# The first norm's modulation by quarters of the features, with the v product behind each quarter

## The chip, the cores and the metric

The kernel runs on one core of one Trainium2 chip. The metric is the time on the device for one execution, in microseconds, here as the median of several runs. Five engines work beside each other: TensorE (PE in the profile) multiplies matrices, VectorE (DVE), ScalarE (ACT) and GpSimd (POOL) do the elementwise work, and SyncE (SP) issues the transfers (DMA) from memory. Each engine takes its instructions in the order of its own queue.

## What is computed

Three blocks of a transformer over 256 tokens of 1024 features, all in float32. The change lies in the beginning of the first one:

```
c_act = silu(c)                                    # one vector of 1024
mod   = c_act @ ada_w[0] + ada_b[0]                # 6 x 1024: sh1, sc1, g1, sh2, sc2, g2
h = rmsnorm(x, norm_g[0, 0]) * (1 + sc1) + sh1     # first norm and its modulation
q, k, v, o, ig, fg = split(h @ a_w_in)             # 512, 512, 1024, 1024, 8, 8
y = mlstm(q, k, v, gates ig and fg)                # 8 heads, chunks of 128 tokens
y = (sigmoid(o) * headnorm(y)) @ a_w_out
x = x + g1 * rmsnorm(y, norm_g[0, 1])              # then sh2, sc2, feed-forward, g2, ...
```

After this come a feed-forward, a second block with a gating unit and its feed-forward, and a third block with attention, a convolution and a mixture of experts. None of them is touched.

## The kernel before

Activations are kept transposed, features on the 128 partitions: `x` is 8 chunks of 128 features by 256 tokens. A float32 product is made of three faster ones: `split` (line 349) cuts an operand into a high part (ScalarE, line 350) and the rest (VectorE, line 351), and `mm3` (line 380) adds high x high, high x low and low x high. `dense_b` (line 392) makes one chunk of 128 output features for 256 tokens with 24 such products over 256 columns. `Acc` (line 54) makes an output with tokens on the partitions, 1024 features wide: 12 products over 512 columns for each of the 8 input chunks, into four PSUM tiles; the last `tail` chunks are held back and then done first for one half of the tokens and then for the other. `weights` (line 359) loads 1 MiB of weights into one of three buffers `st` of the pool `wst` and splits it in two halves.

The modulation vectors come from `ada_w`, 4 MiB each. The two that the first norm needs (sh1 and sc1) are made in `first_block` (line 825) by `ada_start` (line 463), four times 512 features: half of the 8 input chunks are multiplied and summed by VectorE (lines 477 and 479), the other half go through float32 products on TensorE against a replicated vector `crep` (line 481), a float32 product with ones adds the sum over partitions (line 482), and `diagonal` (line 486) picks the columns out of the replicated rows. Then `Finish.whole` (line 243) normalises x, transposes it, applies gain and shift, and runs a `Head` (line 117): float32 products, straight from the unsplit activations, of the 40 gate columns and the first two q chunks (line 135).

`mlstm` (line 584) goes on: gates (tanh, exp, log on ScalarE, then two scans on VectorE, lines 597 to 609), a round trip through memory that spreads the running maximum `M` over the partitions (lines 612 to 615), and its masking on GpSimd. The other q and k chunks follow as split products (lines 624 to 631), then the v product by `dense_a` (line 642), whose four PSUM tiles ScalarE copies to `v` (line 645). Then the o loop (line 694) runs the o product with two heads' scores and sums ahead of each pair of chunks, and the output product ends the block, with the next norm and the feed-forward's float32 head behind it.

The other modulation vectors of the block (g1, sh2, sc2) are side work: generators of steps. `pump(budget)` (line 280) runs steps as long as the budget is above zero; a step that loads 1 MiB and multiplies it on VectorE (line 507) counts 2.4, an adding step with TensorE (lines 535 and 517) 0.6 or 1.3. With a budget of 2.0, `mlstm` calls it after the third and the fourth pair of q and k chunks, four times in the v product and three times in the o loop. `ada_row` also loads a row of `norm_g` and one of the bias. All these loads use the three buffers of `wst`, and the transfers stand in SP's queue in the order in which the program makes them.

The order of the instructions on each engine is not written out by hand, apart from a few places (`issue_after`): a planner sets it before the run, from the order of the program and its own estimates of when an operand is ready.

Of the kernel before, what the change touches and what calls it, by code (L numbers as in the profile page):

```python
# [10 lines left out]
F32 = mybir.dt.float32  # L11
# [6 lines left out]
ALU = mybir.AluOpType  # L18
# [5 lines left out]
KD = 8  # L24
T = 256
# [112 lines left out]
class Finish:  # L138
# [101 lines left out]
            self.run(1)  # L240
            self.split(1)

    def whole(self):

        self.chain(0, None)
        self.turn(0)
        self.end(None)


class Lent:  # L250

# [9 lines left out]
class Net:  # L261
# [198 lines left out]
        return t  # L460


    def ada_start(self, i, b, o):


        nc = self.nc
        s = self.ada_p.tile([128, 1024], F32, tag="ada", name="ada")[:, :512]
        w = self.a["ada_w"][i, b // 2].rearrange("q p (k n) -> q p k n", k=2)[:, :, :, (b % 2) * 512:(b % 2 + 1) * 512]
        ps = self.sd_tile()
        for h in range(2):  # L470
            st = self.wst.tile([128, 2048], F32, tag="st", name="st").rearrange("p (k n) -> p k n", k=4)
            for q in range(2):
                nc.sync.dma_start(st[:, 2 * q:2 * q + 2], w[2 * h + q])
            for k in range(4):
                kk = 4 * h + k
                if kk == 1:
                    nc.vector.tensor_scalar(s, st[:, k], self.cact[:, kk:kk + 1], None, op0=ALU.mult)
                elif k % 2:
                    nc.vector.scalar_tensor_tensor(s, st[:, k], self.cact[:, kk:kk + 1], s, op0=ALU.mult, op1=ALU.add)
                else:  # L480
                    nc.tensor.matmul(ps, self.crep[:, kk], st[:, k], start=kk == 0, stop=False)
        nc.tensor.matmul(ps, self.ones, s, start=False, stop=True)
        self.diagonal(ps, o)
        nc.vector.tensor_tensor(o, o, self.col("ada_b", 48 * i + 4 * b, 4), op=ALU.add)

    def diagonal(self, ps, o):

        nc = self.nc
        d = self.ada_p.tile([128, 4, 128], F32, tag="adad", name="adad", bufs=1)
        nc.vector.tensor_tensor(d, ps.rearrange("p (k c) -> p k c", k=4), self.ident.unsqueeze(1).to_broadcast([128, 4, 128]), op=ALU.mult)  # L490
        nc.vector.tensor_reduce(o, d, axis=AX.X, op=ALU.add)
# [89 lines left out]
        return fin.x  # L581


    def mlstm(self, x, pump, finish):
        nc, a = self.nc, self.a
        with ExitStack() as es:
            mp = es.enter_context(self.tc.tile_pool(name="ml", bufs=1))
# [3 lines left out]
            v = mp.tile([128, 2, 8, 129], F32, name="v")  # L591
            nc.gpsimd.memset(v[:, :, :, 128:129], 1.0)
            one8 = mp.tile([8, T], F32, name="one8")
            nc.gpsimd.memset(one8, 1.0)

            ps = self.head.ps[0]
            b15 = mp.tile([40, 1], F32, name="b15")
            nc.vector.tensor_scalar(b15, self.col("bif")[:40], 1.0 / 15.0, None, op0=ALU.mult)
            th = mp.tile([40, T], F32, name="th")
# [16 lines left out]
            for o in (0, 256):  # L616
                d = mx[:, :, o:o + 128]
# [4 lines left out]

            kT = mp.tile([128, 4, T], F32, name="kT")
            for n2 in range(4):
                for j, ps in enumerate(self.pair(x, a["a_w_qk"], n2, 1)):
                    n = 2 * n2 + j
                    if n < 4:
                        nc.scalar.copy(qz[0:64, 2 * n], ps[0:64])
                        nc.scalar.copy(qz[64:128, 2 * n + 1], ps[64:128])  # L629
                    else:  # L630
                        nc.scalar.mul(kT[:, n - 4], ps, 0.125)
                if n2 == 2:
                    pt = self.sd_tile()
                    for t in range(2):
                        nc.tensor.transpose(pt[:, t * 8:t * 8 + 8], av[:, t * 128:(t + 1) * 128], self.ident[:8, :8])
                        nc.tensor.transpose(pt[:, 16 + t * 8:24 + t * 8], em[:, t * 128:(t + 1) * 128], self.ident[:8, :8])
                    ac = mp.tile([128, 4, 8], F32, name="ac")
                    nc.vector.tensor_copy(ac, pt[:, :32].rearrange("p (a h) -> p a h", a=4))
                if n2 >= 2:
                    self.pump(pump)  # L640

            acc = self.dense_a(x, a["a_w_v"], pump=pump)
            for t in range(2):
                for h in range(2):
                    nc.scalar.copy(v[:, t, 4 * h:4 * h + 4, :128], acc[t][h].rearrange("p (h d) -> p h d", h=4))
            hh = mp.tile([128, 2, 8, 129], F32, name="hh")
            sq = mp.tile([128, 2, 8], F32, name="sq")

# [44 lines left out]
            acc = Acc(self, KD, tail=3)  # L693
# [18 lines left out]
        with self.tc.tile_pool(name="work", bufs=1) as p:  # L712
            fin = finish(p)
# [111 lines left out]
    def first_block(self):  # L825
        with self.tc.tile_pool(name="adap", bufs=2) as self.ada_p, self.tc.tile_pool(name="wsx", bufs=2) as self.wsx:
            m0, first, rest = self.ada_mods(0)
            with self.tc.tile_pool(name="crep", bufs=1) as p:
                self.crep = p.tile([128, KD, 128], F32, name="crep")
                self.nc.vector.tensor_copy(self.crep, self.cact.unsqueeze(2).to_broadcast([128, KD, 128]))  # L830
                for b in range(4):
                    self.ada_start(0, b, m0["sh1" if b < 2 else "sc1"][:, 4 * (b % 2):4 * (b % 2) + 4])
                    if b == 0:
                        self.nc.sync.dma_start(self.X, self.a["x"].rearrange("o (t p) d -> p (o t) d", p=128))
                o = m0["sc1"]
                self.nc.vector.scalar_tensor_tensor(o, o, 1.0, self.col("ng0_0"), op0=ALU.add, op1=ALU.mult)
            with self.tc.tile_pool(name="st0", bufs=2) as p, self.tc.tile_pool(name="work", bufs=1) as work:
                fin = Finish(self, work, None, m0["sc1"], m0["sh1"], head=[(self.a["a_w_g"], 1, 40)] + self.pairs(self.a["a_w_qk"], 2), head_pool=p)
                fin.whole()
# [12 lines left out]
        self.wsx = None  # L852
        return x
# [573 lines left out]
def prep(i):  # L1427
    c = lambda v: np.asarray(v).reshape(-1, 128).T
# [22 lines left out]
    o["norm_g"], o["ada_b"] = i["norm_g"], i["ada_b"]  # L1451

    o["ada_w"] = i["ada_w"].reshape(2, 4, 2, 128, 6, 1024).transpose(0, 4, 1, 3, 2, 5).reshape(2, 6, 4, 128, 2048)
    o["ffn_w1"] = np.stack([_pack_b(w) for w in i["ffn_w1"]])
    o["ffn_w2"] = np.stack([_pack_a(w) for w in i["ffn_w2"]])
    w = i["a_w_in"][0]
    g = np.zeros((1024, 40), f32)
# [4 lines left out]
    w = i["b_w_in"][0]  # L1462
# [5 lines left out]
    w = i["w_in_2"][0]  # L1468
# [37 lines left out]
```

## Time and profile before

| | us |
|---|---|
| median of 3 runs | 1779.6 (1777.91 to 1779.66) |
| profiled execution | 1777.4 |
| its span, first to last instruction | 1775.7 |
| TensorE busy in the span | 1727.9 |
| VectorE busy | 1370.4 |
| ScalarE busy | 865.8 |

The profiled execution is one run, and the times of all rows are its times, counted from the start of its span. A busy time counts an engine's instructions that run, not whether it does useful work at its peak; matrix products overlap, so TensorE's busy time can be read as the time in which it had something to do. The last part of the page follows the chain of work that ended last back from the end of the span; an engine with a large share of it sets the time.

### The profile page before, as it was taken

The page shows a single profiled execution, that of the slowest core. Times are in us where ns is not written, and L with a number is a line of the kernel's source. Part 1 is how long each engine was busy: PE and PEld are TensorE (multiplying, and loading weights), DVE is VectorE, ACT ScalarE, POOL GpSimd, SP SyncE. Part 2 cuts the span into 40 slices and gives each one's busy share as a digit, 9 for nine tenths or more (in the row PEclk, how much of TensorE's full clock was granted, in tenths as well). Part 3 has the DMA queues.
Part 4 walks back from the last instruction along what each step waited for, and adds up shares of the span by engine and source line. Part 5 has one row for each costly group of instructions (what it writes and reads, how often), then busy time and mean ns, then how long its engine had stood idle before and what let it go on. Part 6 is the DMA issues. An engine that isn't in the chain of part 4 may idle for free.

```text
span 1775.7 us, 29680 instructions
## 1 busy us (share of the span) xinstructions
PE 1727.9 (97%) x11986; PEld 1545.4 (87%) x11986; DVE 1370.4 (77%) x2366; ACT 865.8 (49%) x1372; POOL 42.8 (2%) x50
## 2 busy tenths in 40 slices
PE   7999999999999999998999999999999999999998
PEld 3878889887879899898989999999988998888886
DVE  6687887579957655899867999789788958965654
ACT  3565445454545544564645445455444344444644
POOL 0110000000000000002000000000000000000000
PEclk9999999999999999999999999999999999999999
DMA  9874897467827653543436555544555454455751
GB/s 350 307 273 155 326 332 279 165 244 258 292 70 287 240 189 117 197 143 119 146 119 227 175 178 182 184 164 170 172 180 175 147 187 167 167 179 180 264 190 48
DMA packets 59604, 352.51 MB, mean 199 GB/s; under 512 B 6165, under 2 KB 12613, under 8 KB 19273
## 3 DMA queue, kind: packets, MB, share of 16 engines
q1 hardware_dynamic: 59466, 350.61, 56.1%
q8 instruction: 94, 1.54, 0.3%
q14 instruction: 44, 0.36, 0.1%
HBM read 349.51 MB, written 1.07 MB: 197 GB/s over the span
## 4 chain that ended last, share of the span: by engine, by line
PE 85%; DVE 7%; ACT 3%; DMA 2%; issue 2%; POOL 1%; SPq 0%; POOLq 0%; DVEq 0%; ACTq 0%
PE acc L113 38%; PE mm L382 13%; PE mm L384 13%; PE mm L383 13%; PE head L135 2%; DVE lo L351 2%; PE sd L1180 2%; DMA st<-in_ada_w_dram 1%; ACT hi L350 1%; DVE yc L894 1%; ACT junk L162 1%; DMA st<-in_a_w_v_dram 1%; DVE ada L507 1%; POOL rs_r L427 1%; PE sd L799 1%
## 5 line engine op out<-in xcount | busy, mean ns | idle before, releaser
L351 DVE TENSOR_TENSOR lo<-st,hi 128x1024 fp32r<-128x1024 f32 (+1 forms) x507 | 614.8, 1225 | 176.4 <-ACT hi L350 175.1
L350 ACT CAST hi<-st 128x1024 fp32r<-128x1024 f32 (+1 forms) x507 | 523.7, 1048 | 453.1 <-PE mm L383 225.2
L382 PE MATMUL mm<-hhi,hi 128*128 128x256 f32 (+1 forms) x2000 | 575.8, 288 | 0.7 <-ACT qz L629 0.7
L384 PE MATMUL mm<-hhi,lo 128*128 128x256 f32 (+1 forms) x2000 | 566.9, 284 | 8.0 <-DVE lo L351 7.9
L383 PE MATMUL mm<-hlo,hi 128*128 128x256 f32 (+1 forms) x2000 | 567.0, 284 | 0.0
L384 PEld LDWEIGHTS mm<-hhi,lo 128*128 128x128 f32 (+1 forms) x2000 | 383.7, 192 | 9.0 <-DVE lo L351 9.0
L382 PEld LDWEIGHTS mm<-hhi,hi 128*128 128x128 f32 (+1 forms) x2000 | 384.0, 192 | 3.6 <-issue 1.4
L383 PEld LDWEIGHTS mm<-hlo,hi 128*128 128x128 f32 (+1 forms) x2000 | 384.3, 192 | 3.1 <-issue 2.1
L113 PE MATMUL acc<-hi,vh 128*128 128x512 f32 x448 | 141.0, 396 | 0.0
L113 PE MATMUL acc<-lo,vh 128*128 128x512 f32 x448 | 138.3, 390 | 0.0
L113 PE MATMUL acc<-hi,vl 128*128 128x512 f32 x448 | 137.9, 389 | 0.0
L507 DVE SCALAR_TENSOR_TENSOR ada<-st,cact,ada 128x1024 f32<-128x1024 f32 x74 | 95.2, 1287 | 10.1 <-DMA st<-in_ada_w_dram 5.9
L113 PE MATMUL acc<-hi,h 128*128 128x512 f32 x320 | 100.5, 395 | 2.4 <-ACT hi L350 2.4
L113 PE MATMUL acc<-lo,h 128*128 128x512 f32 x320 | 100.4, 394 | 0.1
L113 PE MATMUL acc<-hi,l 128*128 128x512 f32 x320 | 99.9, 393 | 0.0
L113 PEld LDWEIGHTS acc<-hi,vl 128*128 128x128 f32 x448 | 84.1, 188 | 17.9
L113 PEld LDWEIGHTS acc<-lo,vh 128*128 128x128 f32 x448 | 84.1, 188 | 17.9
L113 PEld LDWEIGHTS acc<-hi,vh 128*128 128x128 f32 x448 | 81.6, 188 | 15.0
L350 ACT CAST vh<-gx 128x512 fp32r<-128x512 f32 x64 | 39.9, 624 | 96.2 <-PE acc L113 94.1
L113 PE MATMUL acc<-hi,hhi 128*128 128x512 f32 x224 | 73.6, 406 | 4.0 <-ACT hhi L350 2.1
L113 PE MATMUL acc<-lo,hhi 128*128 128x512 f32 x224 | 72.4, 396 | 1.0 <-DVE lo L351 0.9
L113 PEld LDWEIGHTS acc<-lo,h 128*128 128x128 f32 x320 | 60.3, 189 | 13.7 <-DVE lo L351 1.0
(380 smaller groups left out, 2174.8 us busy)
## 6 DMA issues: line engine op xcount, KB each, us to landing
st<-in_peer_u_dram SPq DMA_DIRECT2D x64, 1024.0 KB, 4.8
st<-in_peer_v_dram SPq DMA_DIRECT2D x64, 1024.0 KB, 4.8
st<-in_ffn_w_dram SPq DMA_DIRECT2D x63, 1024.0 KB, 4.9
st<-in_ada_w_dram SPq DMA_DIRECT2D x40, 1024.0 KB, 5.6
st<-in_ada_w_dram SPq DMA_DIRECT2D x16, 512.0 KB, 7.2
st<-in_b_w_u_dram SPq DMA_DIRECT2D x8, 1024.0 KB, 5.0
st<-in_b_w_v_dram SPq DMA_DIRECT2D x8, 1024.0 KB, 4.8
st<-in_b_w_out_dram SPq DMA_DIRECT2D x8, 1024.0 KB, 5.8
```

What stands on the lines that cost most here:

```text
L113: ins = mm(self.t[t][j], a[:, ts], b[:, j * 512:(j + 1) * 512], start=first and a is xh and b is wh, stop=last and a is xl)
L135: net.nc.tensor.matmul(ps[:, t * 128:(t + 1) * 128], w[:, k], x(k), start=k == 0, stop=k == KD - 1)
L162: nc.scalar.activation(net.junk[:, halves[h]], src, AF.Square, scale=1.0 / 32.0, accum_out=out[:, h:h + 1])
L350: i = self.nc.scalar.copy(hi, src)
L351: return i.ins, self.nc.vector.tensor_tensor(lo, src, hi.bitcast(F32), op=ALU.subtract).ins
L382: mm(out, ahi, bhi, start=start, stop=False)
L383: mm(out, ahi, blo, start=False, stop=False)
L384: return mm(out, alo, bhi, start=False, stop=stop)
L427: nc.gpsimd.tensor_tensor(r, v, m, op=ALU.pow)
L507: nc.vector.scalar_tensor_tensor(s, w, c, s, op0=ALU.mult, op1=ALU.add)
L799: nc.tensor.matmul(ps[:, t], v[:, t, n * 128:(n + 1) * 128], ws[:, n], start=False, stop=t == 1)
L1180: nc.tensor.matmul(pg[:, i], A[:, i // 2, :, i % 2], B[:, c, i // 2, :, i % 2], start=c == 0, stop=c == 1)
```

## The change

`ada_start`, `crep` and `Finish.whole` go, and with them the float32 head of the gates and of the first two q chunks. `mlstm` calls a new function `lead_in`. It loads x in two halves ahead of the weights, normalises and transposes it without a gain, and keeps it as `xT`. Then it goes through four quarters of 256 features. For each it loads 2 MiB of modulation weights, laid out anew (`ada_w0`: shift and gain columns of the quarter side by side, 512 columns, rows of 8 KB), into four buffers of its own pool `st0`. VectorE sums six of the eight input chunks; TensorE adds the other two and the sum over partitions as products with a single column, 12 for a quarter, so that the vectors come out as columns and need no diagonal. Bias and gain are applied to four columns, 1 MiB of v weights is loaded and split, and for the quarter's two chunks of 128 features the modulated value is made over all 256 tokens, split, and added to the v product at once, with a tail of 2.

After that `mlstm` copies v, makes the gates with `dense_b` from split weights (40 columns) and all eight q and k chunks with `dense_b`, and calls `pump` after each of the four pairs. The budget is 3.0 in place of 2.0; there are no calls in the v product any more, and three in the o loop as before.

```diff
+    def lead_in(self):
+        nc, a = self.nc, self.a
+        x = self.h_tiles()
+        acc = Acc(self, KD, tail=2)
+        with self.tc.tile_pool(name="st0", bufs=4) as st0, self.tc.tile_pool(name="xt", bufs=2) as p:
+            src = a["x"].rearrange("o (t p) d -> p (o t) d", p=128)
+            for t in range(2):
+                nc.sync.dma_start(self.X[:, t], src[:, t])
+            xT = p.tile([128, KD, T], F32, name="xT", bufs=1)
+            for t in range(2):
+                fin = Finish(self, p, None, None)
+                fin.chain(t, None)
...
+                        nc.tensor.transpose(ps[:, k], fin.xn[:, kk * 128:(kk + 1) * 128], self.ident)
+                    o = xT[:, 4 * q:4 * q + 4, t * 128:(t + 1) * 128]
+                    if q:
+                        nc.scalar.copy(o, ps)
+                    else:
+                        nc.vector.tensor_copy(o, ps)
+            for f in range(4):
+                s = self.ada_p.tile([128, 1024], F32, tag="ada", name="ada")[:, :512]
+                for h in range(2):
+                    st = self.load(a["ada_w0"][f, h], st0).rearrange("p (k n) -> p k n", k=4)
+                    for k in range(4 - 2 * h):
+                        c = self.cact[:, 4 * h + k:4 * h + k + 1]
+                        if h + k == 0:
+                            nc.vector.tensor_scalar(s, st[:, k], c, None, op0=ALU.mult)
+                        else:
+                            nc.vector.scalar_tensor_tensor(s, st[:, k], c, s, op0=ALU.mult, op1=ALU.add)
+                ps = self.sd_tile()[:, :4]
+                for j in range(4):
+                    js = slice(j * 128, (j + 1) * 128)
+                    for k in (2, 3):
+                        nc.tensor.matmul(ps[:, j:j + 1], st[:, k, js], self.cact[:, 4 + k:5 + k], start=k == 2, stop=False)
+                    nc.tensor.matmul(ps[:, j:j + 1], s[:, js], self.ones[:, :1], start=False, stop=True)
+                m = self.small.tile([128, 4], F32, tag="m0", name="m0")
...
+                nc.vector.tensor_tensor(m.rearrange("p (c k) -> p c k", c=2), ps.rearrange("p (c k) -> p c k", c=2), b, op=ALU.add)
+                g = m[:, 2:4]
+                nc.vector.scalar_tensor_tensor(g, g, 1.0, self.col("ng0_0", 2 * f, 2), op0=ALU.add, op1=ALU.mult)
+                ws = self.weights(a["a_w_v"][f])
+                for j in range(2):
+                    k = 2 * f + j
+                    hf = p.tile([128, T], F32, tag="hf", name="hf")
+                    nc.vector.tensor_scalar(hf, xT[:, k], g[:, j:j + 1], m[:, j:j + 1], op0=ALU.mult, op1=ALU.add)
+                    self.split(x[0][:, k], x[1][:, k], hf)
+                    acc.add((x[0][:, k], x[1][:, k]), ws[j])
+        return x, acc.t
...
-            ps = self.head.ps[0]
+            w = tuple(t.rearrange("p (k m) -> p k m", k=KD) for t in self.weights(a["a_w_g"])[0])
+            ps = self.dense_b(x, w, m=40)
...
-                for j, ps in enumerate(self.pair(x, a["a_w_qk"], n2, 1)):
+                for j, w in enumerate(self.weights_b(a["a_w_qk"][n2])):
+                    ps = self.dense_b(x, w)
...
-                if n2 >= 2:
-                    self.pump(pump)
-
-            acc = self.dense_a(x, a["a_w_v"], pump=pump)
+                self.pump(pump)
...
-            x = self.mlstm(fin.x, 2.0, lambda p: Finish(self, p, m0["g1"], m0["sc2"], m0["sh2"], head=self.pairs(self.a["ffn_w1"][0], 4)))
+            x = self.mlstm(3.0, lambda p: Finish(self, p, m0["g1"], m0["sc2"], m0["sh2"], head=self.pairs(self.a["ffn_w1"][0], 4)))
```

## Rows read from the trace of the kernel before

**Rows 1.** The page: span, busy time and share of each engine, chain by engine.

```profile
span 1775.7 us, 29680 instructions
PE 1727.9 (97%) x11986; PEld 1545.4 (87%) x11986; DVE 1370.4 (77%) x2366; ACT 865.8 (49%) x1372; POOL 42.8 (2%) x50
...
PE 85%; DVE 7%; ACT 3%; DMA 2%; issue 2%; POOL 1%; SPq 0%; POOLq 0%; DVEq 0%; ACTq 0%
```

**Rows 2.** Windows by stage: busy time of each engine, clock, DMA share and rate.

```profile
core 0: us, PE busy (x) PEld busy (x) DVE busy (x) ACT busy (x) POOL busy (x), PEclk, DMA share, GB/s
8.00:32.00 24.00, 21.21 (x52) 7.97 (x50) 15.72 (x28) 4.00 (x10) 1.19 (x2) 1.00 1.03 390
...
8.00:87.50 79.50, 73.65 (x390) 53.25 (x389) 56.42 (x78) 36.21 (x62) 8.24 (x7) 1.00 0.92 340
...
34.76:46.25 11.49, 11.43 (x95) 10.36 (x96) 10.06 (x16) 7.43 (x14) 0.00 (x0) 1.00 0.94 371
46.25:65.05 18.80, 18.14 (x151) 17.79 (x150) 11.76 (x14) 13.55 (x22) 3.92 (x4) 1.00 0.73 248
65.05:91.13 26.08, 25.43 (x110) 19.79 (x109) 18.64 (x16) 12.55 (x19) 3.13 (x2) 1.00 0.96 365
91.13:126.50 35.37, 33.55 (x175) 27.64 (x174) 32.32 (x68) 24.08 (x65) 3.95 (x3) 1.00 0.74 269
126.50:156.90 30.40, 27.41 (x126) 21.12 (x125) 25.20 (x42) 12.66 (x24) 3.07 (x3) 1.00 0.58 208
```

**Rows 3.** Timeline of TensorE: start, length, line, operation, tiles, count.

```profile
65.09 0.63 PE L113 MATMUL acc<-hi,hhi 128*128 128x512 f32 x2
...
91.13 0.94 PE L113 MATMUL acc<-hi,hhi 128*128 128x512 f32 x3
...
156.88 7.30 PE L135 MATMUL head<-hf,st 128*128 128x128 f32 x64
...
167.05 9.04 PE L135 MATMUL head<-hf,st 128*128 128x128 f32 x64 [1.99 <-DVE hf L210]
```

**Rows 4.** By line and shape: count, busy us, mean ns; last by source.

```profile
L351 DVE TENSOR_TENSOR lo<-st,hi 128x1024 fp32r<-128x1024 f32 x506 | 614.1, 1226 | 176.4 <-ACT hi L350 175.1
...
L507 DVE SCALAR_TENSOR_TENSOR ada<-st,cact,ada 128x1024 f32<-128x1024 f32 x74 | 95.2, 1287 | 10.1 <-DMA st<-in_ada_w_dram 5.9 <-DMA ada<-in_ada_b_dram 2.7 <-ACT ada L505 0.8
...
L567 DVE SCALAR_TENSOR_TENSOR s<-mm,r 128x256 f32<-128x256 f32 x57 | 23.9, 419 | 9.7 <-ACT r L565 9.5
...
L479 DVE SCALAR_TENSOR_TENSOR ada<-st,cact,ada 128x512 f32<-128x512 f32 x12 | 9.0, 749 | 3.8 <-DMA st<-in_ada_w_dram 3.7
...
L350 ACT CAST hi<-st 128x1024 fp32r<-128x1024 f32 x506 | 523.0, 1049 | 450.7 <-PE mm L383 222.8 <-PE acc L113 126.5 <-issue 38.8
...
L910 PE MATMUL sd<-kc,qi x16: 166/250/250, 870.3 to 871.9; 128*128 128x1 f32 x16
```

**Rows 5.** DMA, 0 to 8 us: packets and bytes moved.

```profile
DMA packets 1015, 1.72 MB, mean 215 GB/s; under 512 B 206, under 2 KB 334, under 8 KB 1015
```

**Rows 6.** Waits: us in total, times, longest (SP: to 60 us).

```profile
DVE C L605 <- ACT lf L603: 4.4, 1, 4.4
...
SPq L612 <- DVE M L609: 7.1, 1, 7.1
```

**Rows 7.** Timeline of SP's queue: start, length, line, transfer.

```profile
46.57 0.33 SPq L459 DMA_DIRECT2D hnrow<-in_a_hnorm_g_dram  x1
54.04 0.30 SPq L612 DMA_DIRECT2D md<-M  x1
```

**Rows 8.** Tile mx: second exponents, ns min/median/max, first and last start.

```profile
L652 ACT ACTIVATE e<-mx,ac x3: 386/387/403, 68.2 to 68.8; 128x128 f32<-128x128 f32 x3
```

**Rows 9.** Windows: TensorE's granted clock, sixth column after the names.

```profile
164.00:168.00 4.00, 2.01 (x18) 1.77 (x17) 3.82 (x8) 3.97 (x8) 0.00 (x0) 1.00 0.00 0
168.00:172.00 4.00, 4.00 (x23) 4.00 (x23) 2.29 (x3) 0.92 (x2) 0.00 (x0) 0.57 0.49 137
```

**Rows 10.** Timeline of GpSimd: the fill of the zeroed q tile.

```profile
46.60 1.81 POOL L590 MEMSET qz<- 128x2048 f32 x1 [27.97 <-PE head L135]
```

More of the change, by code (lines that the diff above doesn't have):

```diff
@@ L241, in end @@
             self.split(1)
[L243 to L247, printed above, removed]
 class Lent:
@@ L460, in bcast_row @@
         return t
[L463 to L484, printed above, removed]
     def diagonal(self, ps, o):
@@ L581, in ffn @@
         return fin.x
-    def mlstm(self, x, pump, finish):
+    def lead_in(self):
[10 more added lines that the diff above has]
+                fin.chain(t, None)
+                for q in range(2):
+                    ps = (self.sd_tile, self.mm_tile)[q]().rearrange("p (k c) -> p k c", k=4)
+                    for k in range(4):
+                        kk = 4 * q + k
+                        nc.tensor.transpose(ps[:, k], fin.xn[:, kk * 128:(kk + 1) * 128], self.ident)
[21 more added lines that the diff above has]
+                m = self.small.tile([128, 4], F32, tag="m0", name="m0")
+                b = self.col("ada_b", 0, 16).rearrange("p (c k) -> p c k", c=2)[:, :, 2 * f:2 * f + 2]
+                nc.vector.tensor_tensor(m.rearrange("p (c k) -> p c k", c=2), ps.rearrange("p (c k) -> p c k", c=2), b, op=ALU.add)
[9 more added lines that the diff above has]
+        return x, acc.t
@@ L585, in mlstm @@
+    def mlstm(self, pump, finish):
         nc, a = self.nc, self.a
         with ExitStack() as es:
+            v = es.enter_context(self.tc.tile_pool(name="mlv", bufs=1)).tile([128, 2, 8, 129], F32, name="v")
+            nc.gpsimd.memset(v[:, :, :, 128:129], 1.0)
+            x, acc = self.lead_in()
+            for t in range(2):
+                for h in range(2):
+                    nc.scalar.copy(v[:, t, 4 * h:4 * h + 4, :128], acc[t][h].rearrange("p (h d) -> p h d", h=4))
             mp = es.enter_context(self.tc.tile_pool(name="ml", bufs=1))
@@ L590, in mlstm @@
             nc.gpsimd.memset(qz, 0.0)
-            v = mp.tile([128, 2, 8, 129], F32, name="v")
-            nc.gpsimd.memset(v[:, :, :, 128:129], 1.0)
             one8 = mp.tile([8, T], F32, name="one8")
             nc.gpsimd.memset(one8, 1.0)
-            ps = self.head.ps[0]
+            w = tuple(t.rearrange("p (k m) -> p k m", k=KD) for t in self.weights(a["a_w_g"])[0])
+            ps = self.dense_b(x, w, m=40)
             b15 = mp.tile([40, 1], F32, name="b15")
@@ L638, in mlstm @@
                     nc.vector.tensor_copy(ac, pt[:, :32].rearrange("p (a h) -> p a h", a=4))
-                if n2 >= 2:
-                    self.pump(pump)
-            acc = self.dense_a(x, a["a_w_v"], pump=pump)
-            for t in range(2):
-                for h in range(2):
-                    nc.scalar.copy(v[:, t, 4 * h:4 * h + 4, :128], acc[t][h].rearrange("p (h d) -> p h d", h=4))
+                self.pump(pump)
             hh = mp.tile([128, 2, 8, 129], F32, name="hh")
@@ L827, in first_block @@
             m0, first, rest = self.ada_mods(0)
[L828 to L839, printed above, removed]
             self.side = rest[:3]
-            x = self.mlstm(fin.x, 2.0, lambda p: Finish(self, p, m0["g1"], m0["sc2"], m0["sh2"], head=self.pairs(self.a["ffn_w1"][0], 4)))
+            x = self.mlstm(3.0, lambda p: Finish(self, p, m0["g1"], m0["sc2"], m0["sh2"], head=self.pairs(self.a["ffn_w1"][0], 4)))
             m1, first, rest1 = self.ada_mods(1)
@@ L1453, in prep @@
     o["ada_w"] = i["ada_w"].reshape(2, 4, 2, 128, 6, 1024).transpose(0, 4, 1, 3, 2, 5).reshape(2, 6, 4, 128, 2048)
+    w = i["ada_w"][0][:, :2048].reshape(2, 4, 128, 2, 4, 256)
+    o["ada_w0"] = w.transpose(4, 0, 2, 1, 3, 5).reshape(4, 2, 128, 2048)
     o["ffn_w1"] = np.stack([_pack_b(w) for w in i["ffn_w1"]])
```

## The prediction

> **What bounds the kernel now.** I read the page first: TensorE is busy for 97% of the span and holds 85% of the chain that ended last, so outside the start the kernel is as long as its matrix products [rows 1]. The profiled execution took 1777.4 us (span 1775.7 and 1.7 around it); the median of the runs is 1779.6. My differences come from the profile and are taken off the median.
>
> Then the start, in stretches [rows 2]. Up to 34.76 us the loads rule: 390 GB/s over 8 to 32 us, and the 8 MiB of modulation weights must be in before the first normed value exists. From 34.76 to 91.13 TensorE hardly rests: 11.49 us for the float32 head (gates and two q chunks), 18.80 us for the six other q and k chunks, 26.08 us for the v product with four side products and the scores of two heads in between. At 91.13 the first product of the o phase begins, as the products of v had at 65.09 [rows 3]. That is my marker, S: what follows up to the feed-forward's head (91.13 to 156.9) is the same code in both kernels. The 56.4 us between 34.76 and 91.13 are what the change can shorten.
>
> **What it does to TensorE.** The float32 head goes and three split products come: one costs at most 18.80 / 6 = 3.1 us [rows 2], so 9.4 us for 11.5. The v product leaves the stretch and goes under the loads. Nine products of 3.1 us, 28 us, then lie between the end of v and S. The float32 modulation products with their diagonals lay under the loads and lie there again as 48 one-column products; their removal I cost at nothing. The nearest row, 128x128 weights against one column, gives 16 records in 1.6 us [rows 4], which is eight products at 0.2 us, 2.4 us a quarter.
>
> **When v ends.** By their shapes the loads up to the last v weights are constants 0.56, x 1, modulation 8 and v 4 MiB: 14.2 MB. By 8 us 1.72 MB have moved [rows 5]; the other 12.5 MB at 390 GB/s take 32.1 us: 40.1 us. Behind that lie one half's cast (1.05 us) and subtraction (1.23 us) [rows 4] and the last two k chunks of v, a quarter of 26.08: 6.5 us. That is 48.9 us. VectorE may be later: a quarter has six steps over 128x512 (0.75 us each), two modulations and two subtractions over 128x256 (0.42 each, by the nearest row), two weight subtractions (1.23) [rows 4], and two small adds (I estimate 0.4 in all), 9.0 us, against 8.1 us for a quarter's 3 MiB and 2.4 + 6.5 = 8.9 us on TensorE. From 10.5 us, when the first half of a quarter is in, four quarters end at 46.5 and v at 53. I take 51, so by TensorE alone S is 51 + 28 = 79.
>
> **What is late next: the loads.** Weights and side work share three buffers on SP's queue, in program order. Before the o phase's first weights the queue now has, beyond the 14.2 MB, gate weights 0.16 MiB, q and k 4, seven side blocks 7, two rows 1, the decay broadcast 1.5 and the o weights 1. Seven, because a budget of 3 lets two 2.4 steps through per call and the loop calls four times; before it was six, in six calls. Altogether 28.2 MiB or 29.6 MB; 27.9 MB behind 8 us at 390 GB/s are 71.5 us, so the o weights are in at 79.5 if nothing breaks the stream. Before, 8 to 87.5 us ran at 340 GB/s [rows 2], and the largest break was the gate chain: VectorE stood 4.4 us before the scan that waits for ScalarE's logarithm, SP 7.1 us before the store of M [rows 6], and no load was issued between 46.57 and 54.04 us [rows 7], with all three buffers full behind VectorE's queue. The gates now come at 54 us, with that chain unchanged. Its price lies between 0 (buffers empty all the same) and the whole loss against 390, about 11 us; I take the 4.4 us of VectorE, since it is VectorE that frees the buffers. 79.5 + 4.4 + 1.05 + 1.23 = 86.2 us is S, against 91.1: **4.9 us less**. VectorE's own sum agrees: 36 us of quarters, 2 of norm (an estimate), 10 of q and k weights, 18 of side blocks (14 steps of 1.29 us), 6 of gates, fill and row (an estimate), 1.2 for the first o weights, 73 us behind 8, 81, and with the 4.4 us 85.6.
>
> A word on the rate. The trace has 390 GB/s over 24 us [rows 2]. [...]
>
> **The small edits.** The x load goes from behind two blocks to the front, in two halves: 1 MiB earlier, 2.7 us later for the first modulation weights, and within the byte sum. The four v copies move to the end of the lead-in, where ScalarE has some 3 us a quarter to do (two casts of 1.05 us and two short ones): nothing; without that cover less than 1.05 us each. The fill of the zeroed q tile waits for the lead-in's memory and runs beside the gates' 3 us; uncovered it costs 1.8 us [rows 10]. The decay exponents were ready at about 69 us, 23 behind the gates [rows 8]; now 54 + 23 = 77, ahead of S by 9. One side block more is done by S; that is worth between 0 and 2.6 us later, where VectorE is busy for 32.32 of 35.37 us and TensorE stands for 1.8 us there and 3.0 in the next stretch [rows 2]. I take 0, because the o loop's three calls now let four blocks through where they let two.
>
> **Rivals.** *Unbroken loads*: the chain's break falls where buffers are empty anyway. S = 79.5 + 2.3 = 81.8, 9.3 us gained, with the side block up to 11.9: 1770.3, at best 1767.7. For it: TensorE at 79 is no hindrance, and rows of 8 KB take the place of 2 KB pieces. Against: VectorE's sum without a single wait is 81.
>
> *No change*: the loads run as they did from 8 to 87.5, 340 GB/s with all breaks. 27.9 / 0.340 = 82 us, S = 90 + 2.3 = 92.3: 1780.8. For it: that rate held over 80 us with the same queue, the same three buffers and the same chain. Against: two of its breaks were TensorE's own pace holding the buffers. [...]
>
> *Slower: the lead-in runs as a chain.* VectorE's queue is in order. If it stands at each quarter's small add until the twelve one-column products are through (2.4 us), and at the subtraction until ScalarE's cast is done, some 3.5 us a quarter are lost, 14 in all; the buffers fill behind it, so the loads stand too. S = 86.2 + 14 = 100 at the worst, and about 96 where a third of it is covered by the next quarter's steps: 1784.5. It turns to a loss from 1.2 us a quarter (4.9 / 4). [...] For it: the three engines have 8.1, 9.0 and 8.9 us in a quarter, so nothing is spare. Against: two halves of the next quarter stand in four buffers, so VectorE has other work to be given.
>
> *The order changes elsewhere.* Queue order comes from a planner; shifts in later stages could give or take some us either way.
>
> **How the numbers follow.** A run of this kernel tells 0.2%, 3.6 us, from no change. Forecast 0.40 (4.9 us, own range 1771 to 1778: 0.33 faster, 0.07 same); unbroken 0.18 (faster); no change 0.22 (0.17 same, 0.03 slower, 0.02 faster); chain 0.17 (0.15 slower, 0.02 same); elsewhere 0.03 in thirds. Faster 0.54, same 0.27, slower 0.19. Predicted 1779.6 - 4.9 = 1774.7. The range reaches from the unbroken case with its side block (1767) to the middle of the chain case (1784).
>
> **What would show it.** In the trace of the changed kernel: the last v product ends at 49 to 53 us (past 56 is the chain); loads at 385 GB/s or more from 8 to 40 (360 or less: the no-change case); TensorE then waits for weights, not weights for TensorE, with 4 to 8 us of gaps between 55 and S, ended by the casts of q, k and o weights; S near 86; VectorE idle about 4 us before the scan; the stretch from S to the feed-forward's head 63 to 66 us long. S below 83 shows the unbroken case, S at 90 to 93 no change. The forecast is wrong if S moves and the head doesn't, or if v ends on time and S doesn't move.

## The result: 1802.3 us, 22.7 us slower, and where it went

| | before | after |
|---|---|---|
| median of the runs, us | 1779.5 (1777.9 to 1779.7) | 1802.3 (1801.8 to 1802.4) |
| ratio, 95% interval | | 1.0131 (1.0117 to 1.0146) |
| span of the profiled execution, us | 1775.7 | 1800.5 |
| last v product ends, us | 90.5 | 73.9 |
| first o product (S), us | 91.1 | 117.5 |
| first product of the feed-forward's head, us | 156.9 | 183.8 |
| from there to the end of the span, us | 1618.8 | 1616.7 |

The head is 26.9 us late, and what follows is 2.1 us shorter: the loss lies in the first 184 us. The page of after, beside [rows 1], shows little of it; TensorE is still busy for 96% of the span:

```profile
span 1800.5 us, 29745 instructions
...
PE 1733.9 (96%) x12018; PEld 1561.7 (87%) x12018; DVE 1375.3 (76%) x2377; ACT 866.9 (48%) x1373; POOL 41.7 (2%) x50
...
PE 86%; DVE 7%; ACT 3%; issue 2%; POOL 1%; DMA 0%; SPq 0%; POOLq 0%; DVEq 0%; ACTq 0%
```

The windows by stage do, beside [rows 2]. They reach to 32 us (389 GB/s where it was 390), to the end of the v product, to S and to the head (columns as there; the last is GB/s):

```profile
8.00:32.00 24.00, 15.73 (x59) 13.80 (x60) 15.09 (x26) 7.12 (x15) 1.09 (x2) 1.00 0.95 389
32.00:73.90 41.90, 34.09 (x152) 28.56 (x152) 22.99 (x40) 11.37 (x18) 2.04 (x2) 0.76 0.42 160
73.90:117.50 43.60, 35.56 (x233) 32.66 (x231) 29.13 (x30) 20.69 (x36) 4.74 (x2) 0.84 0.80 292
117.50:183.80 66.30, 61.57 (x296) 48.62 (x297) 55.62 (x106) 36.62 (x88) 6.14 (x6) 1.00 0.64 232
```

The last row is the same 66 us as before. From 32 to 73.9 us, while v is made, every resource is slack: 160 GB/s, VectorE busy for 23.0 of 41.9 us, TensorE at 0.76 of its clock and idle for 7.8 us. No engine is full and the loads are not either, which is the sign of a chain of waits. In the text, v(f) stands for the v products of quarter f, and the one-column products are those that end a quarter's modulation vectors. Here is one quarter on TensorE (start, length, line, operation, count; in brackets the idle time before):

```profile
25.29 2.07 PE L113 MATMUL acc<-hi,hhi 128*128 128x512 f32 x4 [2.60 <-ACT hi L344]
27.16 1.05 PE L113 MATMUL acc<-lo,hhi 128*128 128x512 f32 x2
...
32.72 0.61 PE L113 MATMUL acc<-hi,hlo 128*128 128x512 f32 x2
33.17 0.50 PE L594 MATMUL sd<-cact,st 128*128 128x1 f32 x4
...
38.51 2.08 PE L113 MATMUL acc<-hi,hhi 128*128 128x512 f32 x4 [2.60 <-ACT hi L344]
```

The same quarter on VectorE (L598 is the small add of a quarter's modulation, L589 its sums):

```profile
22.72 0.16 DVE L598 TENSOR_TENSOR m<-sd,cols 128x4 f32<-128x4 f32 x1 [4.52 <-PE sd L595]
...
28.06 3.90 DVE L589 SCALAR_TENSOR_TENSOR ada<-st,cact,ada 128x512 f32<-128x512 f32 x5
35.94 0.16 DVE L598 TENSOR_TENSOR m<-sd,cols 128x4 f32<-128x4 f32 x1 [3.98 <-PE sd L595]
```

and on ScalarE (the casts of the modulated values, then of the v weights):

```profile
36.78 0.73 ACT L344 CAST hhi<-hf 128x256 fp32r<-128x256 f32 x2 [10.60 <-DVE hf L605]
37.42 1.99 ACT L344 CAST hi<-st 128x1024 fp32r<-128x1024 f32 x2
```

Read it round. TensorE makes v(f) from 25.29 to 33.17 (7.9 us), then the one-column products of quarter f + 1 to 35.9 (2.7). VectorE's small add has stood for them since 31.96 and goes at 35.94. Modulation, the cast of the values and the cast of the weights follow, 2.6 us in which TensorE stands, and v(f + 1) begins at 38.51. That makes 7.9 + 2.7 + 2.6 = 13.2 us a quarter, and 13.4 and 13.5 in the next two. The waits, summed from 8 to 120 us (us in total, times, longest):

```profile
DVE m L598 <- PE sd L595: 17.0, 4, 4.5
...
PE acc L113 <- ACT hi L344: 10.4, 4, 2.6
...
SPq L350 <- DVE lo L345: 40.0, 6, 13.0
```

VectorE stands 17.0 us at the four small adds, TensorE 10.4 us ahead of the four quarters of v, and SP, in this longer stretch, 40 us for buffers that VectorE has not yet emptied. Two closed rounds of waits, called rings here, run through this. TensorE's ring is the one above. VectorE's ring is its own work from one small add to the end of the next sums (22.72 to 31.96, 9.2 us) and the one-column products behind them. The second comes to 9.2 + 2.7 = 11.9 us, 1.3 below the first.

### The profile page after: what moved, and what is told of

The parts are those of the page before. It is cut to its first block, busy times and chain, and to the rows that moved or that the text cites. A ratio compares the mean times of both kernels' runs of the same rounds, so it can differ in the third digit from the quotient of the medians.

```text
span 1800.5 us, 29745 instructions
## 1 busy us (share of the span) xinstructions
PE 1733.9 (96%) x12018; PEld 1561.7 (87%) x12018; DVE 1375.3 (76%) x2377; ACT 866.9 (48%) x1373; POOL 41.7 (2%) x50
## 4 chain that ended last, share of the span: by engine, by line
PE 86%; DVE 7%; ACT 3%; issue 2%; POOL 1%; DMA 0%; SPq 0%; POOLq 0%; DVEq 0%; ACTq 0%
PE acc L113 39%; PE mm L376 13%; PE mm L378 13%; PE mm L377 13%; DVE lo L345 2%; PE head L135 2%; PE sd L1195 2%; ACT hi L344 1%; DVE ada L478 1%; DVE yc L909 1%; ACT junk L162 1%; PE sd L826 0%; PE sd L488 0%; POOL rs_r L421 0%; ACT hhi L344 0%
## 5 line engine op out<-in xcount | busy, mean ns | idle before, releaser
L376 PE MATMUL mm<-hhi,hi 128*128 128x256 f32 (+1 forms) x2024 | 584.9, 289 | 0.6 <-ACT hi L344 0.6
L378 PE MATMUL mm<-hhi,lo 128*128 128x256 f32 (+1 forms) x2024 | 575.7, 285 | 9.3 <-DVE lo L345 9.2
L377 PE MATMUL mm<-hlo,hi 128*128 128x256 f32 (+1 forms) x2024 | 575.5, 284 | 0.0
L378 PEld LDWEIGHTS mm<-hhi,lo 128*128 128x128 f32 (+1 forms) x2024 | 389.6, 193 | 10.9 <-DVE lo L345 10.8
L376 PEld LDWEIGHTS mm<-hhi,hi 128*128 128x128 f32 (+1 forms) x2024 | 390.0, 193 | 4.7 <-ACT hi L344 1.7
L377 PEld LDWEIGHTS mm<-hlo,hi 128*128 128x128 f32 (+1 forms) x2024 | 390.1, 193 | 3.5 <-issue 2.3
L113 PEld LDWEIGHTS acc<-hi,vl 128*128 128x128 f32 x448 | 84.1, 188 | 17.9
L113 PEld LDWEIGHTS acc<-lo,vh 128*128 128x128 f32 x448 | 84.1, 188 | 17.9
L113 PE MATMUL acc<-hi,hhi 128*128 128x512 f32 x224 | 76.3, 424 | 13.3 <-ACT hi L344 11.8
L113 PE MATMUL acc<-lo,hhi 128*128 128x512 f32 x224 | 75.9, 413 | 0.6 <-DVE lo L345 0.5
L113 PE MATMUL acc<-hi,hlo 128*128 128x512 f32 x224 | 74.2, 406 | 0.1
```

The costliest lines, as they stand in the source:

```text
L113: ins = mm(self.t[t][j], a[:, ts], b[:, j * 512:(j + 1) * 512], start=first and a is xh and b is wh, stop=last and a is xl)
L376: mm(out, ahi, bhi, start=start, stop=False)
L377: mm(out, ahi, blo, start=False, stop=False)
L378: return mm(out, alo, bhi, start=False, stop=stop)
```

## Experiments

Each is the changed kernel with one edit or with several of them together, but for split_head, which is the kernel before with one. *Quarter* is the time between small adds (in sched and sched_b2 that of the first three adds; the last quarter is shorter), *v* the end of the last v product, *head* the feed-forward's first product; the runs of the kernel before are those on the same chip. The medians there differ by up to 1.7 us, so where it matters a gain is given beside the kernel before on the same chip, against the 22.7 us that after loses to it.

| run | median us | before | ratio (95%) | quarter | v | head |
|---|---|---|---|---|---|---|
| after | 1802.3 | 1779.5 | 1.0131 (1.0117 to 1.0146) | 13.2 to 13.5 | 73.9 | 183.8 |
| v_last | 1824.4 | 1778.8 | 1.0254 (1.0233 to 1.0274) | 13.8 | 89.2 | 206.4 |
| sums_first | 1790.4 | 1778.7 | 1.0059 (1.0038 to 1.0080) | 11.1 to 12.3 | 68.8 | 172.2 |
| sched | 1786.5 | 1778.8 | 1.0042 (1.0025 to 1.0059) | 9.15 | 61.4 | 167.6 |
| casts_first | 1797.8 | 1778.7 | 1.0106 (1.0084 to 1.0128) | 11.6 to 12.5 | 68.1 | 181.2 |
| pe_filled | 1809.8 | 1778.8 | 1.0172 (1.0151 to 1.0192) | 13.9 to 14.8 | 76.6 | 187.7 |
| pe_filled_2 | 1799.4 | 1777.9 | 1.0123 (1.0106 to 1.0140) | 11.7 to 11.9 | 67.4 | 180.0 |
| budget_2 | 1796.8 | 1778.8 | 1.0099 (1.0079 to 1.0119) | 13.7 | 75.9 | 181.5 |
| sched_b2 | 1784.2 | 1778.7 | 1.0028 (1.0019 to 1.0038) | 9.15 | 61.7 | 167.2 |
| gates_first | 1785.5 | 1779.0 | 1.0037 (1.0023 to 1.0051) | | 64.5 | 166.6 |
| gates_first_b2 | 1783.1 | 1779.0 | 1.0027 (1.0016 to 1.0038) | | 64.5 | 166.5 |
| gates_first_b2_all | 1784.2 | 1779.0 | 1.0027 (1.0017 to 1.0037) | | 64.2 | 164.5 |
| split_head | 1782.6 | 1778.7 | 1.0027 (1.0015 to 1.0038) | | | 162.7 |

**v_last** takes v out of TensorE's ring: the products of v wait for their quarter's operands in a list and run at the end.

```diff
-        acc = Acc(self, KD, tail=2)
+        acc = Acc(self, KD, tail=8)
...
-                    acc.add((x[0][:, k], x[1][:, k]), ws[j])
+                    with self.tc.issue_after(last.ins):
+                        acc.add((x[0][:, k], x[1][:, k]), ws[j])
```

> The changed kernel with all 96 products of v placed behind the last quarter's one-column products in TensorE's queue. Theory A (the quarters run as one ring: products of v, one-column products of the next quarter behind them, add, modulation, casts, next products of v; 13.2 us a round): the first three quarters come apart from v, VectorE waits some 3 us for the one-column products in place of 4.3, a quarter takes 11 to 12 us, the last modulation ends near 60 and v, 22 us long, near 82 instead of 73.9. Theory B (the loads, held up by buffers, set the round): a quarter stays at 13 us.

The quarter did not shorten: 13.8 us, and v's 25 us came behind. VectorE's timeline shows why:

```profile
36.83 0.16 DVE L598 TENSOR_TENSOR m<-sd,cols 128x4 f32<-128x4 f32 x1 [4.52 <-PE sd L595]
...
42.16 3.90 DVE L589 SCALAR_TENSOR_TENSOR ada<-st,cact,ada 128x512 f32<-128x512 f32 x5
50.58 0.16 DVE L598 TENSOR_TENSOR m<-sd,cols 128x4 f32<-128x4 f32 x1 [4.52 <-PE sd L595]
```

From the small add to the end of the sums it is 9.2 us, then VectorE stands 4.5 us for one-column products, with no v product near. So v(f), queued ahead of them, is not all that makes the quarter long: VectorE's ring goes on without it. It is as long as before only because the one-column products take 4.5 us here for 2.7 in after; at 2.7 it would be 11.9 (an estimate from the two). The expectation would have read a quarter of 13 us as the loads' doing; sched, below, which has the same loads and buffers, rules that out.

**sums_first** opens VectorE's ring and leaves TensorE's, a little shorter: the sums of f + 1 stand ahead of f's small add, and the weights' casts ahead of the values'.

```diff
+                if f < 3:
+                    s, st, d = sums(f + 1)
+                    wn = self.weights(a["a_w_v"][f + 1])
...
+                with self.tc.issue_after(d.ins), self.tc.issue_after(sub), self.tc.issue_after(cast):
                     nc.vector.tensor_tensor(m.rearrange("p (c k) -> p c k", c=2), ps.rearrange("p (c k) -> p c k", c=2), b, op=ALU.add)
...
+                if f < 3:
+                    with self.tc.issue_after(acc.last.ins):
+                        ws, ps = wn, columns(s, st)
```

> The changed kernel with VectorE's order as in the run called sched (sums of quarter f+1 and its weights' casts ahead of quarter f's small add), but TensorE's order as in the changed kernel: the v products of quarter f ahead of the one-column products of quarter f+1. It separates two rings. TensorE's ring (v products, then one-column products, then small add, modulation and cast, then v products again) is left: 5.9 to 7.7 us + 2.8 + some 1.8 = 10.5 to 12.3 us a quarter, v ends near 67, 1790 to 1794 us. If VectorE's ring alone set the 13.2 us (9.2 us of its own work and then the stand for the one-column products), a quarter is now 9.2 us as in sched, v ends near 61, 1785 to 1788.

A quarter is 11.1 to 12.3 us, as TensorE's ring has it, and the time is 11.1 us nearer to the kernel before.

**sched** opens both: as sums_first, and the one-column products of f + 1 ahead of v(f) (the edit is shown against sums_first).

```diff
-                if f < 3:
-                    with self.tc.issue_after(acc.last.ins):
-                        ws, ps = wn, columns(s, st)
+                with self.tc.issue_after(cur[2].ins):
+                    for j in range(2):
+                        k = 2 * f + j
+                        acc.add((x[0][:, k], x[1][:, k]), ws[j])
```

> The changed kernel with the ring cut by order alone: VectorE makes the sums of quarter f+1 and subtracts its weights ahead of the small add of quarter f, ScalarE casts the weights ahead of the activations, TensorE makes the one-column products of f+1 ahead of v of f. Theory A: 8.5 to 9.5 us a quarter, v ends at 53 to 57, time lower by 15 to 20 us than the changed kernel (1782 to 1787). Theory B: no change in the round, 1802.

The loss falls from 22.7 to 7.6 us, by order alone. VectorE no longer stands at the first three adds (no bracket):

```profile
34.44 0.15 DVE L608 TENSOR_TENSOR m<-sd,cols 128x4 f32<-128x4 f32 x1
...
39.78 3.90 DVE L588 SCALAR_TENSOR_TENSOR ada<-st,cact,ada 128x512 f32<-128x512 f32 x5
43.60 0.15 DVE L608 TENSOR_TENSOR m<-sd,cols 128x4 f32<-128x4 f32 x1
```

9.15 us a quarter is VectorE's own work, with a wait of 0.5 for a cast; the prediction had it at 9.0. So the loads did not set the 13.2 us, and the two rings did: a quarter is 13.8 us with TensorE's opened (there with slower one-column products), 11.1 to 12.3 with VectorE's opened, 9.15 with both.

**casts_first** only exchanges ScalarE's casts, weights ahead of values.

```diff
+                ws = self.weights(a["a_w_v"][f])
+                cast = self.hi
                 m = self.small.tile([128, 4], F32, tag="m0", name="m0")
...
+                    with self.tc.issue_after(cast):
+                        self.split(x[0][:, k], x[1][:, k], hf)
```

> The changed kernel with one exchange on ScalarE: the two casts of the v weights ahead of the two of the modulated values, where they stood behind them. Both rings stay as they are. Theory of the two rings: the stand of TensorE ahead of each quarter's v products falls from 2.6 us to some 1.3, a quarter from 13.2 to about 12 (VectorE's ring, 9.2 + 2.8, then sets it), 4 to 5 us in all: 1797 to 1798. If that stand is hidden by something else: no difference, 1802.

TensorE's stand fell from 2.6 to 1.3 us, as expected:

```profile
35.43 1.22 PE L113 MATMUL acc<-hi,hhi 128*128 128x512 f32 x2 [1.34 <-ACT hhi L344]
```

The quarter falls to about 12 us, the length of VectorE's ring, which is still closed. The time is 4.5 us lower (3.7 beside the kernel before; the intervals overlap). Beside sums_first this run tells more. The stand is 1.3 us in both, and v ends at 68.1 us here and 68.8 there; yet the head comes 9 us later here. What differs ahead of that is the loads, which wait for buffers that VectorE frees (40.0 us of such waits in after, above). The second load of q and k weights is issued in sums_first at

```profile
57.93 0.35 SPq L350 DMA_DIRECT2D st<-in_a_w_qk_dram  x1
```

and in casts_first at

```profile
66.53 0.35 SPq L350 DMA_DIRECT2D st<-in_a_w_qk_dram  x1
```

So much of what sums_first gained does not come from the end of v.

**pe_filled** and **pe_filled_2** fill TensorE's stand with idle products, five and two a quarter, to hold its clock.

```diff
+                fill = self.mm_tile()
+                with self.tc.issue_after(last.ins):
+                    for r in range(5):
+                        nc.tensor.matmul(fill, self.ident, self.X[:, 0, :512], start=r == 0, stop=r == 4)
```

> The changed kernel with five idle float32 products (2.6 us) behind each quarter's one-column products, so that TensorE does not stand before the v products. If the half clock after each stand costs what it seems to (24 products in 7.65 us in place of 5.5), a round falls from 13.2 to about 11.1 us, v ends near 66 instead of 73.9 and the time falls by 7 to 8 us. If the ring is held by loads or by VectorE, v ends where it did and the time stays within 2 us.

> pe_filled with two idle float32 products behind each quarter's one-column products in place of five. In pe_filled the five took 5.7 us where TensorE's stand is 2.6 us, so a quarter grew from 13.2 to 14.4 us, while its v products, at full clock, took 5.9 us for 7.65. Two take some 2.3 us and fit into the stand. If the half clock is part of the ring, a quarter is 12 us (VectorE's ring, 9.2 + 2.8, then sets it), v ends 4 to 5 us earlier and the time is 1797 to 1799. If two products don't hold the clock, or the clock is no part of it: 1802 to 1804.

Five were a miss by size: a quarter grew to between 13.9 and 14.8 us. They ran 5.7 us where the stand was 2.6, and no run shows five of them in 2.6 us (pe_filled):

```profile
38.33 6.23 PE L599 MATMUL mm<-X,kc 128*128 128x512 f32 x10
44.00 1.03 PE L113 MATMUL acc<-hi,hhi 128*128 128x512 f32 x2
```

Two fit (pe_filled_2):

```profile
35.12 1.96 PE L599 MATMUL mm<-X,kc 128*128 128x512 f32 x4
37.87 1.21 PE L113 MATMUL acc<-hi,hhi 128*128 128x512 f32 x4 [0.78 <-ACT hi L344]
```

Behind that first row the v products take 0.73 and then 0.62 us a pair, where after has 1.05 for some five microseconds; the quarter falls to 11.8 us and v ends 6.5 us sooner. The granted clock in the three windows of 8 us from 32 to 56 us is 1.00, 0.99 and 0.80, where after has 0.82, 0.76 and 0.67. The slower v products were part of TensorE's ring. But the head comes only 3.8 us sooner, and the time falls by 2.9 (1.2 beside the kernel before, well within the intervals): most of it is given back behind v.

**budget_2** and **sched_b2** take the kernel before's budget for side work, 2.0 at two of the four calls.

```diff
-                self.pump(pump)
+                if n2 >= 2:
+                    self.pump(pump)
...
-            x = self.mlstm(3.0, lambda p: Finish(self, p, m0["g1"], m0["sc2"], m0["sh2"], head=self.pairs(self.a["ffn_w1"][0], 4)))
+            x = self.mlstm(2.0, lambda p: Finish(self, p, m0["g1"], m0["sc2"], m0["sh2"], head=self.pairs(self.a["ffn_w1"][0], 4)))
```

> The changed kernel with the side work's budget back at 2.0 and called after the third and fourth q and k pair alone, as before: two side blocks ahead of the o weights in place of seven. Theory A: v ends at 73.9 all the same; S comes up to 8 us earlier than 117.5, and most of that is given back behind S, where the blocks then lie: time lower by 0 to 4 us. Theory C (the crowded queue of loads is the main loss): time lower by more than 10 us.

> The run called sched with the side work's budget and calls of the kernel before (2.0, and only at the last two of the four q and k pairs). In the changed kernel that budget gave 5.4 us. If what it gives comes behind v, where both kernels stand for loads and VectorE, it adds up: 1780 to 1782, level with the kernel before. If the budget only helped because v ended late there: 1786. If fewer side steps here mean more of them in the later stages: above 1787.

This gives 5.5 us in after and 2.3 in sched (4.8 and 2.2 beside the kernel before; both pairs of intervals overlap): it does not add up as expected. What it moves is clear. From the end of v to S, and from S to the head, sched:

```profile
61.40:101.70 40.30, 33.44 (x232) 29.91 (x229) 24.59 (x27) 22.35 (x40) 4.79 (x2) 0.92 0.79 288
101.70:167.60 65.90, 61.57 (x297) 48.62 (x298) 55.18 (x105) 35.29 (x84) 6.13 (x6) 1.00 0.64 229
```

sched_b2:

```profile
61.40:89.60 28.20, 27.77 (x229) 27.18 (x226) 16.70 (x18) 19.58 (x34) 4.87 (x2) 1.00 0.73 262
89.60:167.20 77.60, 65.65 (x302) 51.11 (x302) 68.08 (x118) 36.88 (x89) 7.58 (x7) 0.97 0.70 251
```

S moves from 101.7 to 89.6, ahead even of the 91.1 before, and the head from 167.6 to 167.2. The side work in the q and k products is worth 12 us of S and 0.4 of the head. In budget_2, where v ends as late as in after (75.9), the stretch from v to S is as short:

```profile
75.90:104.70 28.80, 27.86 (x229) 27.19 (x227) 16.45 (x19) 19.66 (x34) 4.78 (x2) 1.00 0.82 295
```

**gates_first**, **gates_first_b2**, **gates_first_b2_all** put the gates' product ahead of v(3) in sched, at a budget of 3.0 at all four calls, of 2.0 at two, of 2.0 at all four.

```diff
+                if f == 3:
+                    w = tuple(t.rearrange("p (k m) -> p k m", k=KD) for t in self.weights(a["a_w_g"])[0])
+                    gates = self.dense_b(x, w, m=40)
                 with self.tc.issue_after(cur[2].ins):
```

> The run called sched, with the gate weights' product ahead of the last quarter of v on TensorE (it needs all of x, as that quarter does), so that ScalarE's and VectorE's gate chain runs beside 6 us of v products. In sched VectorE stood 6.0 us before the scan that waits for the logarithm, and no load was issued from 57.4 to 60.8 and to 70.3 us, the buffers being full. Theory: that chain is what makes the stretch from the end of v to the o phase 40 us for the 28 of TensorE's own work; without it the feed-forward's head begins up to 6 us earlier, 1780 to 1783. Rival: the stretch is bound by loads and VectorE's side steps all the same: 1785 to 1787.

> gates_first with the budget and calls of the kernel before (2.0, at the last two of the four q and k pairs). From sched to sched_b2 these gave 2.3 us. If the gate chain gives up to 6 and the two add up: 1778 to 1781, level with the kernel before. If the side steps that no longer run before the o phase set the feed-forward's head, as they do in sched_b2 (o phase to head 77.6 us where it is 65.9 in sched): 1783 to 1785, no better than sched_b2.

> gates_first with a budget of 2.0 at all four q and k pairs (one side block a call there, where 3.0 lets two through and the kernel before has none at the first two): half of the side work of gates_first ahead of the o phase, the rest behind. If the side work's place sets the time, it lies below both neighbours by 1 to 3 us, since neither of the stretches is overfull: 1777 to 1780. If its place doesn't matter: between them.

The scan that waits for the logarithm begins at 63.1 us where it began at 68.1 in sched, and the time falls by 1 us, within the intervals: the rival held. The wait went elsewhere. VectorE's and TensorE's waits in gates_first (us in total, times, longest):

```profile
DVE C L651 <- ACT lf L649: 6.5, 1, 6.5
...
PE sd L506 <- DVE ada L478: 5.6, 1, 5.6
```

VectorE stands as long as before, only earlier; TensorE now stands 5.6 us for a side block's last product, which is queued ahead of the q and k products. With less side work gates_first_b2 is no better than sched_b2, as its second expectation had it, and gates_first_b2_all lies between its neighbours and not below them, so the forecast of 1777 to 1780 for it failed. The three versions lie between 1783 and 1786 us, all still above the kernel before.

**split_head** is the kernel before with one part of the change: gates and two q chunks as split products.

```diff
+        self.x = self.net.h_tiles()
+        self.split(0)
...
-            ps = self.head.ps[0]
+            w = tuple(t.rearrange("p (k m) -> p k m", k=KD) for t in self.weights(a["a_w_g"])[0])
+            ps = self.dense_b(x, w, m=40)
...
-                for j, ps in enumerate(self.pair(x, a["a_w_qk"], n2, 1)):
+                for j, w in enumerate(self.weights_b(a["a_w_qk"][n2])):
+                    ps = self.dense_b(x, w)
...
```

> The kernel before with one part of the change alone: gates and two q chunks as split products in place of the float32 head; modulation, order of v and budget as before. The prediction put TensorE at 9.4 us for 11.5 there, 2.1 less: 1777 to 1778 if that part is as it was forecast. Rival: the split products can begin only when all of x is split and the gate weights are cast, some 2 us later than the float32 products began, so 1779 to 1781.

Slower by 3.9 us, worse than the rival. TensorE's waits from 33 to 66 us (us in total, times, longest):

```profile
PE mm L384 <- ACT hhi L352: 5.5, 1, 5.5
PE mm L201 <- ACT xn L190: 1.0, 1, 1.0
PE mm L385 <- DVE hlo L353: 0.7, 1, 0.7
```

The float32 head began at 34.76 us, chunk by chunk and 128 tokens at a time behind the modulation. The split products take all 256 tokens at once and stand until 41.18, when the second 128 tokens are modulated and their first cast is done; the gate product then takes 5.6 us, at a granted clock of 0.58 (41 to 47 us).

## Why the prediction was wrong

The forecast was 1774.7 us, 4.9 less than before, and 1802.3 came.

**The bound and the marker.** Right that the first 157 us decide: from the head on the two spans are within 2.1 us. Right that S to the head keeps its length with about the same side work ahead of it (66.3 us; 63 to 66 were named). S alone is no marker once side work changes places: sched_b2 has it earlier than before and is slower.

**When v ends: the failed step.** The prediction put loads (8.1 us), VectorE (9.0) and TensorE (8.9) of a quarter side by side and took about the longest: v at 51 us. Measured 73.9. VectorE's term was right (9.15 in sched), the one-column products took 2.7 us for 2.4, and v(f) 7.9 for 6.5, its first products at nearly twice the length after each stand (1.05 us a pair, then 0.62). What was wrong is the operation: these times were to be added round a ring, since each quarter's small add stood ahead of the next quarter's sums on VectorE, and each v(f) ahead of the next one-column products on TensorE. "Two halves of the next quarter stand in four buffers, so VectorE has other work to be given" was the reason against the chain. From 8 to 74 us VectorE waits for no load, so the data were there, but the order had that work behind the waiting add. VectorE kept to the order of its queue: it stood 4.0 to 4.5 us at each of the first three small adds with the next sums queued behind. Even in sched v ends at 61.4: a quarter of 9.15 whose sums run one quarter ahead puts the last small add at 50.2, and v(2) and v(3) follow from 50.0 at 5.7 us each. That is 10 us past the forecast with both rings open.

**The chain rival.** Right in place and in kind, with VectorE standing at the small add (17.0 us of it) and 3.5 us a quarter priced for a measured 4.1 to 4.4 (13.2 to 13.5 against 9.15). It failed in the sum: a third was taken as hidden by the next quarter's steps, none was; TensorE's lower clock was not priced (0.57 granted from 168 to 172 us of the kernel before [rows 9], 0.50 from 41.9 to 43.0 in after); and v itself was left out of the round. S = 100 was called the worst, and it was 117.5. "Past 56 is the chain" told it at once; "loads at 385 or more from 8 to 40" misled: 8 to 32 us ran at 389 GB/s and 32 to 40 at 263, which is 358 from 8 to 40, the sign of the no-change case, though sched shows that no rate was at fault.

**Loads behind v.** The forecast let 27.9 MB run at 390 GB/s to 79.5 us. By 73.9 us the windows add up to 1.8 + 9.3 + 6.7 = 17.9 MB; before, at 340 GB/s from 8 us [rows 2], it was about 24. SP could not run ahead, its three buffers being full behind VectorE, as had happened once in the kernel before [rows 7]. So much was still to be loaded behind v, and v to S took 43.6 us where 35 were forecast. But that stretch does not go by v's lateness alone: with five side blocks less in it (budget_2) it is 28.8 us though v ends as late, and in sched, with the seven, 40.3 though v ends 12.5 us sooner. The price of the seven side blocks there was a term that the sum of bytes had too low.

**The gate chain.** 4.4 us were taken between 0 and 11. VectorE stood 5.1 us in after; gates_first moved the whole chain 5 us forward for 1 us of time, within the intervals, but the stand itself stayed (6.5 us), so what the chain costs is not shown.

**TensorE's head.** 9.4 us for 11.5 was a gain of 2.1, and the edit alone cost 3.9 us instead in the kernel before. The term counted products and left out that a split product waits for the casts of all 256 tokens (5.5 us in split_head). In after that wait does not arise: the gates' products follow v without a stand and take 2.8 us, 3.1 by the forecast.

**Small edits.** The fill of the q tile (1.81 us at 65.0) was waited for by nobody, as forecast. The side block more, taken at 0 between 0 and 2.6 us, was sized too low if anything: the old budget gave 5.5 us back in after and 2.3 in sched, neither clear of the intervals.

**What stays open.** sched removes 15.1 of the 22.7 us. Where the 4 to 8 us come from that it and its variants are still above the kernel before is not shown. split_head's 3.9 us belong to the old order, and the stand that goes with them is not there in after. Where VectorE's ring stays closed, v's gains are given back behind it (casts_first: v 5.8 us sooner, head 2.6), and where it is opened they are not (sums_first: 5.1 and 11.6). The load times beside each other in casts_first and sums_first speak for the buffers that VectorE frees, but no run changed the buffers alone.

## What to carry to other kernels

When a change breaks one stage into steps that pass from engine to engine, write each engine's queue down for one whole step and the next, and follow the waits round until they close: the period is the longest closed round, and busy times only bound it from below. Where two rounds are nearly equal, undoing one may show little, so undo both before you drop the theory. Look for such a round wherever every engine and the loads are slack at once.

## What was not expected of the hardware

**Loads.** From 8 to 24 us after moves 427 GB/s. The DMA view of that stretch, most packets of 8 KB or more:

```profile
DMA packets 937, 6.84 MB, mean 427 GB/s; under 512 B 100, under 2 KB 100, under 8 KB 105
```

and of the kernel before, every packet under 8 KB:

```profile
DMA packets 2998, 6.31 MB, mean 394 GB/s; under 512 B 175, under 2 KB 175, under 8 KB 2998
```

The changed kernel moves 8% more in the same 16 us. Whether the larger packets are the cause is not shown, since no run changed them alone.

**TensorE's clock after a short stand.** After 2.6 us of standing in each quarter the v products ran some 5 us at 1.05 us a pair, then at 0.62; between 41.9 and 43.0 us the granted clock is 0.50. It does not always show this: from 25.3 to 30.0 us the products are as slow, and it reads 1.00. One-column products are the same: in sched six records take 1.28 us from 25.9 us and 0.67 from 38.2 us (after v products), and the granted clock reads 1.00 for both stretches. Why it does not show the slow ones is open. Nor is the stand shown to be the cause: in sched v's pairs take 1.06 us again from 41.75 us, and TensorE had run without a stand since 25.4 us. Two rows of the one-column products, on TensorE's timeline of sched:

```profile
25.88 0.99 PE L593 MATMUL sd<-cact,st 128*128 128x1 f32 x4
...
38.23 0.58 PE L593 MATMUL sd<-cact,st 128*128 128x1 f32 x4
```
